# Half-width tiles for the state-space diagonal products, and later turns for the convolution's channels

## The chip, the core and the metric

The kernel runs on one core of a Trainium2 chip. The metric is the device time of one execution in microseconds (us), the median of several executions. Lower is better. The five engines of the core run side by side, each through its own list of instructions in order, and wait for each other by semaphores: TensorE (PE in the profile; PEld is its loading of the stationary operand), VectorE (DVE), ScalarE (ACT), GpSimd (POOL) and SyncE (SP), whose list here issues the transfers between the chip's memory and the core.

## What is computed

One layer of a hybrid decoder block on a sequence of 1024 tokens with 1024 features, in float32: a token-mixing sub-layer (stick-breaking attention beside a Mamba-2 state-space mixer), a cross-attention sub-layer and a gated feed-forward sub-layer. The change touches two places of the mixer, the causal convolution that makes its inputs and the "diagonal" product inside each chunk of 128 tokens:

```python
xbc = lax.conv_general_dilated(xbc, conv_w[:, None, :], window_strides=(1,),
    padding=[(SSM_CONV - 1, 0)], dimension_numbers=('NWC', 'WIO', 'NWC'),
    feature_group_count=SSM_CONV_DIM)
xbc = jax.nn.silu(xbc + conv_b)
xs, bm, cm = _split(xbc, (SSM_INNER, SSM_GROUPS * SSM_STATE, SSM_GROUPS * SSM_STATE))
...
cb = jnp.einsum('bclgn,bcsgn->bcgls', cc, bc)
y_diag = jnp.einsum('bcgls,bcgels,bcsgep->bclgep', cb, decay, xc)
states = jnp.einsum('bclgn,bcgel,bclgep->bcgepn', bc, decay_to_end, xc)
y_off = jnp.einsum('bclgn,bcgepn,bcgel->bclgep', cc, prev_states, jnp.exp(a_cs))
return (y_diag + y_off).reshape(b, l, h, p)
```

There are 2048 channels of x, in 32 heads of 64, and 512 channels each of B and C, in 4 groups; a group serves 8 heads. A sequence is 8 chunks.

## The kernel before

A float32 operand of a dense product is split into a high and a low part (the float32r type), and a product is three passes of the array: high by high, high by low, low by high. `acc3` (L211) does this over four blocks of the inner dimension, so one call is 12 passes of 512 columns.

**The projections with the convolution (from about 0.27 to 0.64 ms).** 18 pairs of 128-feature blocks are projected by a seven-product Strassen-Winograd scheme, `winograd_pair` (L222). Its first three products open three sums in PSUM: `pa_` with b11, `pc_` with t1, `pb_` with b21. The remaining four (t2, b22, t3, t4) add to `pa_` and `pc_`, and between them ACT and DVE copy or add the sums into the two output tiles `y`: the sum of the first product is copied out (L228) before t2 may add to it, that of the second (L230) before b22. The weights of a pair are loaded by SP, summed on POOL (L183 to L186), and split by ACT (L98) and DVE (L101). The PSUM pool has six rooms for these sums, that is two pairs, so TensorE's order lays the first half of a pair between the halves of the pair before.

Twelve of the 18 pairs are convolution pairs. For each of its two blocks `conv` (L659) takes the finished `y`, runs the four taps (ACT L661, three on DVE L663), the sigmoid (ACT L664) and the product (POOL L665) into a tile `acc`. The 20 blocks that hold x and B are then turned: `tail` (L647) transposes `acc` in eight 128x128 pieces on TensorE (L653) into two PSUM tiles `tr` (a pool of two), which ACT copies (L655) and SP stores (L656) to `xs_d` or `bt_d`. The other six pairs are gate pairs (`gate`, L673): a sigmoid and a store. `y` and `acc` take their rooms in turn from the pool `t4` of six, tag `b4`.

`pair` (L677) puts a pair together: weights, `y`, the seven products, then the turns of every block that is waiting in `pend` (filled by the pair before), then the copy of the last sum (L686) and the convolution or the gate. The order of each engine's list is made by a scheduler when the kernel is built, from the order of the source, the dependencies and its own estimates; `behind` (L204) forbids it to issue instructions ahead of a marked one. The last pair is a gate pair. At its place the last turn waiting is put behind the last product.

**The state-space chunks (about 1.10 to 1.43 ms).** 32 steps (4 groups by 8 chunks) run in a software pipeline: `prep` two steps ahead makes the decay matrices (`dec`, L1087, and `seg`, on ACT and DVE), `states` one step ahead updates the running state (`pst`), `outp` (L1120) makes the output, `flip` two steps behind turns it (`ptr`). Between them stand pieces of the memory projections and of `branch`, the output projection of the mixer (`mm<-oth`), which serve as filling for TensorE. In `outp`, the product with the earlier state is `po` (three passes of 512 columns), and the diagonal product is `pd`: for each of 8 heads the stationary operand is that head's 128x128 matrix in `seg`, and the moving operand a slice of `xs` in plain float32. The array takes a plain float32 product in two passes, so a step has 16 passes of `pd`. The slice of a head is its 64 columns and, except for head 0, the 32 columns before them; the heads run from 7 down to 0, so that what a product wrote too far down is written over by the next one.

Of the kernel before, what the change touches and what calls it, by code (L numbers as in the profile page):

```python
# [8 lines left out]
F32 = mybir.dt.float32  # L9
# [7 lines left out]
P = 128  # L17
S = 1024
# [3 lines left out]
HALF = 512  # L22
# [3 lines left out]
NH, HD = 16, 64  # L26
NG, GH = 4, 8
# [7 lines left out]
def hybrid_block(ctx, tc, a, out, dbg=None):  # L35
    nc = tc.nc
    V, A, G, T = nc.vector, nc.scalar, nc.gpsimd, nc.tensor
# [11 lines left out]
    def mk(pl, shape, dt, tag, bufs=None):  # L49
        uid[0] += 1  # L50
        kw = {} if bufs is None else {"bufs": bufs}
        return pl.tile(shape, dt, tag=tag, name=f"{tag}_{uid[0]}", **kw)
# [151 lines left out]
    def behind(marks):  # L204

        st = ExitStack()
        for m in marks:
            st.enter_context(tc.issue_after(m.ins))
        return st

    def acc3(ps, w, b, first, last, tiles=None):  # L211

        for k in range(4):
            bh, bl = (b[0][:, k, :], b[1][:, k, :]) if tiles is None else tiles[k]
            T.matmul(ps, w[0][:, k, :], bh, start=first and k == 0, stop=False, skip_group_check=True)  # L215
            T.matmul(ps, w[0][:, k, :], bl, start=False, stop=False, skip_group_check=True)  # L216
            ins = T.matmul(ps, w[1][:, k, :], bh, start=False, stop=last and k == 3, skip_group_check=True)  # L217
        return ins

    ends = []  # L220

    def winograd_pair(psp, ws, hb, y):  # L222


        wa11, ws1, ws2, wa12, ws3, ws4, wa22 = ws
        pa_, pc_ = mk(psp, [P, HALF], F32, "mm"), mk(psp, [P, HALF], F32, "mm")
        acc3(pa_, wa11, hb["b11"], True, False)
        A.activation(y[0][0], pa_, AF.Copy)  # L228
        acc3(pc_, ws1, hb["t1"], True, False)
        A.activation(y[1][1], pc_, AF.Copy)  # L230
        acc3(pa_, ws2, hb["t2"], False, False)
        A.activation(y[0][1], pa_, AF.Copy)
        pb_ = mk(psp, [P, HALF], F32, "mm")
        acc3(pb_, wa12, hb["b21"], True, True)
        V.tensor_tensor(y[0][0], y[0][0], pb_, ALU.add)
        acc3(pa_, ws3, hb["t3"], False, False)
        V.tensor_tensor(y[1][1], y[1][1], pa_, ALU.add)
        acc3(pc_, ws4, hb["b22"], False, True)
        V.tensor_tensor(y[0][1], y[0][1], pc_, ALU.add)
        ends.append(acc3(pa_, wa22, hb["t4"], False, True))  # L240
        return pa_
# [7 lines left out]
    with ExitStack() as pa:  # L249
        hp_ = pool(pa, "hT")  # L250
        hb = {n: tuple(mk(hp_, [P, 4, HALF], F32R, n + s) for s in "hl") for n in HB}
# [22 lines left out]
        with ExitStack() as p1:  # L274
# [7 lines left out]
            t4 = pool(p1, "t4x0", 4)  # L282
            tt = pool(p1, "tcomb", 6)
            psp = pool(p1, "ps1", 2, PSUM)
# [141 lines left out]
        with ExitStack() as p1:  # L426
# [4 lines left out]
            psp = pool(p1, "psz", 4, PSUM)  # L431
# [198 lines left out]
        with ExitStack() as p1:  # L630
# [3 lines left out]
            t4 = pool(p1, "t4b", 6)  # L634
            t2 = pool(p1, "t2c", 2)
            dts = mk(pool(p1, "dts"), [P, 2, S // 4], F32, "dts")
            psp = pool(p1, "psx0", 6, PSUM)
# [4 lines left out]
                    yield r.rearrange("p k b f -> p k (b f)"), w_in[kh * 512:(kh + 1) * 512, c0:c0 + 2 * P].rearrange("(k p) f -> p k f", p=P)  # L642
                return loads

            pend = []

            def tail(f, acc):  # L647
                dst = xs_d[f // 4][:, (f % 4) * P:(f % 4 + 1) * P] if f < 16 else bt_d[f - 16]
                for half in range(2):
                    pt = mk(ps1, [P, HALF], F32, "tr")  # L650
                    for c in range(4):
                        cc = half * 4 + c
                        T.transpose(pt[:, c * P:(c + 1) * P], acc[:, cc * P:(cc + 1) * P], ident)  # L653
                    st = mk(t2, [P, HALF], F32, "b2")
                    A.activation(st, pt, AF.Copy)  # L655
                    nc.sync.dma_start(dst[half * HALF:(half + 1) * HALF].rearrange("(c p) f -> p c f", p=P),  # L656
                                      st.rearrange("p (c f) -> p c f", f=P))
# [18 lines left out]

            def pair(c0, f, fin, npool):  # L677
                ws = winograd_weights(rp, sfp, swp, adjacent(c0), npool)
                y = [mk(t4, [P, S], F32, "b4") for _ in range(2)]
                ys = [[t[:, 0:HALF], t[:, HALF:S]] for t in y]  # L680
                p = winograd_pair(psp, ws, hb, ys)
                while pend:

                    with behind(ends[-1:] if f == gts[-1][1] and len(pend) == 1 else []):
                        tail(*pend.pop(0))
                A.activation(ys[1][0], p, AF.Copy)  # L686
                fin(f, y[0])
                fin(f + 1, y[1])

            jobs = [(C_X + f * P, f, conv) for f in list(range(16, 24, 2)) + list(range(0, 16, 2))]  # L690
            gts = [(C_GA + f * P, f, gate) for f in range(0, 16 - LATE_GATES, 2)]
# [21 lines left out]
            for i, j in enumerate(order):  # L713
                if i == 2:
                    dt_columns()
                pair(*j, 3 if i == 0 else 0)
            while pend:
                tail(*pend.pop(0))

            b12 = tuple(mk(hp_, [P, 4, HALF], F32R, "t1" + s) for s in "hl")  # L720
            for i in range(2):
# [14 lines left out]
        with ExitStack() as p2:  # L736
# [17 lines left out]
            marks, sig = [], []  # L754
# [174 lines left out]
            for m in range(NM):  # L929
                h, half = m // 2, m % 2  # L930
                hp, r = m // 4, m % 4
# [21 lines left out]
    with ExitStack() as p3:  # L953
# [8 lines left out]
        t4 = pool(p3, "s4p", 3)  # L962
# [27 lines left out]
        marks = []  # L990
# [129 lines left out]
        def outp(n):  # L1120
            g, c = divmod(n, NCH)
            d, gd = chk[n], grp[g]
            rows_ = slice(c * P, (c + 1) * P)
            seg, xs = d["seg"], d["xs"]
            zs = mk(t2, [P, HALF], F32, "s2")
            nc.sync.dma_start(zs, zs_d[rows_, g * HALF:(g + 1) * HALF])
            y = mk(t2, [P, HALF], F32, "s2")
            G.tensor_tensor(v3(y), v3(xs), dsk[:, g * GH:(g + 1) * GH].unsqueeze(2).to_broadcast([P, GH, HD]), ALU.mult)
            if c > 0:
                po = mk(ps, [P, HALF], F32, "po")  # L1130
                mm3(po, d["ch"], d["cl"], *gd["st", c], True, True)
                yo = mk(t2, [P, HALF], F32, "s2")
                V.tensor_tensor(v3(yo), v3(po), bc(eam, c, g), ALU.mult)
                G.tensor_tensor(y, y, yo, ALU.add)

            pd = mk(ps, [P, HALF], F32, "pd")
            for h in range(GH - 1, -1, -1):
                hs = slice(max(0, h * HD - 32), (h + 1) * HD)
                ins = T.matmul(pd[:, hs], seg[:, h, :], xs[:, hs], start=True, stop=True)
                if h == GH - 1:  # L1140
                    marks.append(ins)
            V.tensor_tensor(y, y, pd, ALU.add)
            V.tensor_tensor(y, y, zs, ALU.mult)
            junk = mk(jk, [P, HALF], BF16, "junk")
            ms = mk(stats, [P, 1], F32, "ms")
            A.activation(junk, y, AF.Square, scale=float(HALF) ** -0.5, accum_out=ms)

            A.activation(y, y, AF.Copy, scale=rstd_of(ms))
            d["y"] = y
# [176 lines left out]
    with ExitStack() as p4:  # L1326
# [16 lines left out]
        for i, (half, k) in enumerate((half, k) for half in range(2) for k in range(KT)):  # L1343
# [3 lines left out]
            t, t_ = [mk(t2, [P, HALF], F32, "m2") for _ in range(2)]  # L1347
# [12 lines left out]
        for f in range(KT):  # L1360
            whi, wlo, _ = first if f == 0 else branch_weights(f)
# [18 lines left out]
    marks = []  # L1380
# [29 lines left out]
    t4 = pool(xt4, "t4x", 3)  # L1410
    psx = ExitStack()
    psp = pool(psx, "psx", 2, PSUM)
# [41 lines left out]
    with ExitStack() as q2:  # L1454
# [17 lines left out]
        for m in range(2):  # L1472
            t = mk(t4, [P, D], F32, "x4")
# [81 lines left out]
    with ExitStack() as q4:  # L1555
# [22 lines left out]
        b11, b21 = hf[0]  # L1578
# [308 lines left out]
```

## Time and profile before

| | |
|---|---|
| Median of 3 executions | 2576.5 us (2574.12 to 2578.33) |
| The profiled execution: its own time | 2577.68 us |
| The profiled execution: span from first to last instruction | 2575.9 us |
| Mean granted TensorE clock | 0.993 |
| Busy: DVE, ACT, POOL | 1797.3 us (70%), 1132.1 us (44%), 852.9 us (33%) |

The profile is that of one execution. A busy time adds up the recorded durations of an engine's instructions. A matmul pass is recorded from its start to a modelled end, about 0.39 us for 512 columns, while the next one starts 0.23 us after it; the cost of a pass in a full stream is therefore read from the distance of starts, and a stop of TensorE from a distance that is longer than that. In a timeline the columns are start, duration, engine, line, operation, tiles, shapes and count; the bracket tells how long the engine was idle before, and who released it. A shape such as 128*64 gives the rows and columns of the array that the instruction uses.

### The profile page before, as it was taken

How to read it: one execution, taken by the hardware profiler on the slowest of the kernel's cores; microseconds unless marked ns; L12 is line 12 of the kernel's file. 1: busy time of each engine (PE TensorE's matmuls, PEld its weight loads, DVE VectorE, ACT ScalarE, POOL GpSimd, SP SyncE). 2: the span in 40 equal slices, each digit the busy share in tenths (PEclk: the TensorE clock that was granted, in tenths of full speed). 3: DMA queues.
4: the chain of work that ended last, by engine and by line, in shares of the span. 5: the costliest groups of instructions: out<-in, count | busy, mean ns of one | idle time of the engine just before them, and what ended most of it. 6: DMA issues, size and time to landing. Idle time of an engine off the chain costs nothing. (4 is left out here: it accounts for less than half of the span.)

```text
span 2575.9 us, 32333 instructions
## 1 busy us (share of the span) xinstructions
PE 2487.7 (97%) x11866; PEld 2057.5 (80%) x11866; DVE 1797.3 (70%) x2093; ACT 1132.1 (44%) x2023; POOL 852.9 (33%) x650
## 2 busy tenths in 40 slices
PE   7999999999999999998999999999999999999998
PEld 5788887887888878787888778887787888888876
DVE  7665777767577887697888664416459666666997
ACT  5333454554556665565554312314333333334343
POOL 3221644444112111254655050101114333323762
PEclk9999999999999999999999999999999999999999
DMA  7441433333443433365332572311232232224232
GB/s 245 150 127 58 147 121 98 105 106 107 134 111 90 119 100 98 107 205 159 104 93 79 171 237 74 131 49 34 98 111 70 78 95 74 90 90 164 99 131 98
DMA packets 255272, 293.44 MB, mean 114 GB/s; under 512 B 17024, under 2 KB 175241, under 8 KB 254987
## 3 DMA queue, kind: packets, MB, share of 16 engines
q1 hardware_dynamic: 255114, 291.40, 36.3%
q8 instruction: 93, 1.52, 0.2%
q14 instruction: 65, 0.52, 0.1%
HBM read 200.10 MB, written 74.45 MB: 107 GB/s over the span
## 5 line engine op out<-in xcount | busy, mean ns | idle before, releaser
L861 DVE TENSOR_TENSOR_SCAN n<-n,mask 128x128 f32<-128x128 f32 (+7 forms) x128 | 187.9, 1494 | 23.4 <-ACT n L860 22.1
L101 DVE TENSOR_TENSOR sw<-sf,sw 128x512 fp32r<-128x512 f32 x150 | 126.3, 855 | 69.5 <-ACT sw L98 69.2
L878 ACT ACTIVATE wth<-tr,mone 128x512 fp32r<-128x512 f32 x192 | 110.6, 585 | 82.9 <-PE tr L875 81.0
L98 ACT ACTIVATE sw<-sf 128x512 fp32r<-128x512 f32 x150 | 91.9, 626 | 108.6 <-PE mm L217 95.2
L183 POOL TENSOR_TENSOR sf<-wr,wr 128x512 f32<-128x512 f32 x38 | 60.1, 1582 | 237.6 <-DMA wr<-in_w_gu_dram 114.5
L879 DVE SCALAR_TENSOR_TENSOR wtl<-tr,wth 128x512 fp32r<-128x512 f32 x192 | 99.6, 544 | 49.8 <-ACT wth L878 49.7
L101 DVE TENSOR_TENSOR sw<-wr,sw 128x512 fp32r<-128x512 f32 x113 | 110.6, 980 | 27.3 <-ACT sw L98 27.2
L217 PE MATMUL mm<-h,sw 128*128 128x512 f32 x320 | 125.0, 392 | 1.8 <-DVE sw L101 1.8
L215 PE MATMUL mm<-h,sw 128*128 128x512 f32 x320 | 122.6, 391 | 2.9 <-ACT h L98 2.3
L216 PE MATMUL mm<-h,sw 128*128 128x512 f32 x320 | 125.3, 391 | 0.0
L98 ACT ACTIVATE sw<-wr 128x512 fp32r<-128x512 f32 x113 | 70.8, 629 | 120.9 <-PE mm L217 120.2
L663 DVE SCALAR_TENSOR_TENSOR b<-b,prmT,b 128x1023 f32<-128x1023 f32 (+2 forms) x72 | 107.4, 1494 | 11.1 <-ACT b L661 10.4
L94 POOL TENSOR_SCALAR v<-va 128x512 fp32r<-128x512 f32 x16 | 20.6, 1288 | 283.8 <-PE av L888 166.0
L860 ACT ACTIVATE n<-sc 128x512 f32<-128x512 f32 (+1 forms) x192 | 88.7, 494 | 45.5 <-PE tr L875 28.7
L152 POOL TENSOR_SCALAR rstd<-ms 128x1 f32<-128x1 f32 x74 | 26.4, 356 | 239.2 <-ACT x L1398 112.2
L104 PE MATMUL mm<-oth,bw 128*128 128x512 f32 x256 | 103.6, 405 | 1.4 <-DVE a L1198 1.3
L104 PE MATMUL p<-bw,h 128*128 128x512 f32 x256 | 98.9, 391 | 3.3 <-DVE x L1400 2.4
L106 PE MATMUL mm<-oth,bw 128*128 128x512 f32 x256 | 100.8, 394 | 0.1
L105 PE MATMUL mm<-otl,bw 128*128 128x512 f32 x256 | 100.5, 393 | 0.0
L106 PE MATMUL p<-bw,h 128*128 128x512 f32 x256 | 100.1, 392 | 0.0
L185 POOL TENSOR_TENSOR sf<-wr 128x512 f32<-128x512 f32 x38 | 63.4, 1668 | 110.3 <-DVE sw L101 110.3
L105 PE MATMUL p<-bw,h 128*128 128x512 f32 x256 | 99.8, 390 | 0.0
(616 smaller groups left out, 8101.3 us busy)
## 6 DMA issues: line engine op xcount, KB each, us to landing
wr<-in_w_gu_dram SPq DMA_DIRECT2D x80, 256.0 KB
wr<-in_w_in_dram SPq DMA_DIRECT2D x36, 512.0 KB
zr<-in_w_in_dram SPq DMA_DIRECT2D x28, 512.0 KB
gu_d<-t SPq DMA_DIRECT2D x44, 256.0 KB
wraw<-in_w_in_dram SPq DMA_DIRECT2D x20, 512.0 KB
zs_d<-zo SPq DMA_DIRECT2D x32, 256.0 KB
xs_d<-b SPq DMA_DIRECT2D x32, 256.0 KB
kl<-gt SPq DMA_DIRECT2D x64, 128.0 KB
```

What stands on the lines that cost most here:

```text
L98: A.activation(o, i, AF.Copy)
L101: eng.tensor_tensor(o, i, hi.bitcast(F32), ALU.subtract)
L104: first = T.matmul(ps, sh, mh, start=start, stop=False)
L105: T.matmul(ps, sh, ml, start=False, stop=False)
L106: T.matmul(ps, sl, mh, start=False, stop=stop)
L215: T.matmul(ps, w[0][:, k, :], bh, start=first and k == 0, stop=False, skip_group_check=True)
L216: T.matmul(ps, w[0][:, k, :], bl, start=False, stop=False, skip_group_check=True)
L217: ins = T.matmul(ps, w[1][:, k, :], bh, start=False, stop=last and k == 3, skip_group_check=True)
L663: V.scalar_tensor_tensor(acc[:, sh:], y[:, :S - sh], cw(3 - sh, f), acc[:, sh:], ALU.mult, ALU.add)
L861: V.tensor_tensor_scan(nt[:, 0:L][:, ::-1], nt[:, 0:L][:, ::-1], mask[:, S - L:][:, ::-1], 1.0, ALU.mult, ALU.max)
L878: A.activation(wh[:, t0 * P:], pt[:, t0 * P:], AF.Identity, bias=mone)
L879: V.scalar_tensor_tensor(wl[:, t0 * P:], pt[:, t0 * P:], -1.0, wh[:, t0 * P:].bitcast(F32), ALU.add, ALU.subtract)
```

## The change

**Convolution.** `winograd_pair` gets a callback. When it is given, the first three products are issued ahead of any copy, and the callback gets the last pass of the third. It puts the turns of the blocks that are `ripe` behind that pass, makes the waiting blocks (`pend`) ripe for the next pair, and only then takes the rooms for `y`. The turns of a convolution pair thus stand behind the third product of the second pair that follows, not after the products of the first pair that follows. The last pair still turns what is left.

**Diagonal product.** Each head's product is cut in two by output rows: columns 0 to 63 of the head's matrix are the stationary operand of one product, which writes PSUM partitions 0 to 63, and columns 64 to 127 that of another, which writes partitions 64 to 127. The moving slice is the 64 columns of the head alone.

```diff
-    def winograd_pair(psp, ws, hb, y):
+    def winograd_pair(psp, ws, hb, y, between=None):
         wa11, ws1, ws2, wa12, ws3, ws4, wa22 = ws
         pa_, pc_ = mk(psp, [P, HALF], F32, "mm"), mk(psp, [P, HALF], F32, "mm")
         acc3(pa_, wa11, hb["b11"], True, False)
+        if between is not None:
+            acc3(pc_, ws1, hb["t1"], True, False)
+            pb_ = mk(psp, [P, HALF], F32, "mm")
+            y = between(acc3(pb_, wa12, hb["b21"], True, True))
         A.activation(y[0][0], pa_, AF.Copy)
-        acc3(pc_, ws1, hb["t1"], True, False)
+        if between is None:
+            acc3(pc_, ws1, hb["t1"], True, False)
         A.activation(y[1][1], pc_, AF.Copy)
         acc3(pa_, ws2, hb["t2"], False, False)
         A.activation(y[0][1], pa_, AF.Copy)
-        pb_ = mk(psp, [P, HALF], F32, "mm")
-        acc3(pb_, wa12, hb["b21"], True, True)
+        if between is None:
+            pb_ = mk(psp, [P, HALF], F32, "mm")
+            acc3(pb_, wa12, hb["b21"], True, True)
         V.tensor_tensor(y[0][0], y[0][0], pb_, ALU.add)
...
-            pend = []
+            pend, ripe = [], []
...
             def pair(c0, f, fin, npool):
                 ws = winograd_weights(rp, sfp, swp, adjacent(c0), npool)
-                y = [mk(t4, [P, S], F32, "b4") for _ in range(2)]
-                ys = [[t[:, 0:HALF], t[:, HALF:S]] for t in y]
-                p = winograd_pair(psp, ws, hb, ys)
-                while pend:
-
-                    with behind(ends[-1:] if f == gts[-1][1] and len(pend) == 1 else []):
-                        tail(*pend.pop(0))
+                y, ys = [], []
+
+                def turns(third):
+                    for t in ripe:
+                        with behind([third]):
+                            tail(*t)
+                    ripe[:] = pend
+                    pend.clear()
+                    y.extend(mk(t4, [P, S], F32, "b4") for _ in range(2))
+                    ys.extend([t[:, 0:HALF], t[:, HALF:S]] for t in y)
+                    return ys
+
+                p = winograd_pair(psp, ws, hb, None, turns)
+                if f == gts[-1][1]:
+                    for i, t in enumerate(ripe):
+                        with behind(ends[-1:] if i == len(ripe) - 1 else []):
+                            tail(*t)
                 A.activation(ys[1][0], p, AF.Copy)
...
-            while pend:
-                tail(*pend.pop(0))
...
             for h in range(GH - 1, -1, -1):
-                hs = slice(max(0, h * HD - 32), (h + 1) * HD)
-                ins = T.matmul(pd[:, hs], seg[:, h, :], xs[:, hs], start=True, stop=True)
-                if h == GH - 1:
-                    marks.append(ins)
+                hs = slice(h * HD, (h + 1) * HD)
+                for j in range(2):
+                    r = slice(j * HD, (j + 1) * HD)
+                    ins = T.matmul(pd[r, hs], seg[:, h, r], xs[:, hs], start=True, stop=True)
+                    if h == GH - 1 and j == 0:
+                        marks.append(ins)
```

## The prediction, made before the changed kernel ran

> **What bounds the kernel now.** I read the page's totals first, then the busy time of the engines by stretches, then TensorE's timeline in the two stages that the change touches.
>
> ```profile
> span 2575.9 us, 32333 instructions
> PE 2487.7 (97%) x11866; PEld 2057.5 (80%) x11866; DVE 1797.3 (70%) x2093; ACT 1132.1 (44%) x2023; POOL 852.9 (33%) x650
> ```
>
> ```profile
> 427.80:431.20 3.40, 3.40 (x10) 2.62 (x9) 1.99 (x3) 3.40 (x7) 0.60 (x1) 0.50 0.61 153
> 345.00:650.00 305.00, 297.28 (x1368) 245.55 (x1367) 220.81 (x207) 161.29 (x244) 141.23 (x75) 0.99 0.36 111
> 1140.00:1180.00 40.00, 35.07 (x185) 28.79 (x184) 35.55 (x39) 22.89 (x39) 22.29 (x21) 1.00 0.58 186
> 1300.00:1340.00 40.00, 40.00 (x224) 34.40 (x223) 36.27 (x46) 19.48 (x38) 22.48 (x20) 1.00 0.31 87
> ```
>
> The columns of the second fence are the stretch, then the busy time of PE, PEld, DVE, ACT and POOL, then the granted clock, DMA share and GB/s. TensorE is the bound: 97% of the span, 297.28 of 305 us in the convolution, all of 40 us in the middle of the chunks. So a pass of the array added or saved there, or a stop removed, goes to the end almost whole. Two exceptions matter. From 1140 to 1180, VectorE (35.55 of 40) is as full as TensorE (35.07); a saved pass is worth little there. From 1300 to 1340 VectorE has 36.27 of 40, so TensorE can gain some 9% before VectorE binds.
>
> **The diagonal products.** Where the sixteen passes of one chunk stand, their loads, and the only half-width passes in the kernel:
>
> ```profile
> 1310.44 0.39 PE L106 MATMUL po<-sth,cl 128*128 128x512 f32 x1
> 1310.67 1.89 PE L1139 MATMUL pd<-s,s 128*128 128x96 f32 x16
> ...
> 1320.25 1.89 PE L1139 MATMUL pd<-s,s 128*128 128x96 f32 x16
> ```
>
> ```profile
> 1310.44 1.98 PEld L1139 LDWEIGHTS pd<-s,s 128*128 128x128 f32 x16
> 1312.34 0.19 PEld L104 LDWEIGHTS mm<-oth,bw 128*128 128x128 f32 x1
> ```
>
> ```profile
> L1139 PEld LDWEIGHTS pd<-s,s x512: 186/192/333, 1101.9 to 1427.3; 128*128 128x128 f32 x171
> L1139 PE MATMUL pd<-s,s x512: 243/275/421, 1102.1 to 1427.4; 128*128 128x96 f32 x149, 128*128 128x64 f32 x22
> ...
> L406 PEld LDWEIGHTS pdt<-b11h,wds x4: 133/134/135, 45.4 to 49.1; 128*64 128x64 f32 x4
> ```
>
> From the first load to the one behind the sixteenth are 1312.34 - 1310.44 = 1.90 us. The first load has to let the 512-column pass of `po` by (1310.67 - 1310.44 = 0.23), so the other fifteen distances are 1.67 / 15 = 0.111 us. A pass of 96 columns is far shorter than the 0.23 of 512, so I read 0.111 as the time to load 128 stationary columns: the loads, not the streaming, set the pace. All of it is 512 x 0.111 = 57 us.
>
> The change makes 256 products of two passes into 512 of two, 1024 passes, each with 64 stationary columns. A load of 64 columns is recorded with 134 ns against 192 for 128, so 58 ns less; against the 189 of other full loads, as at 1312.34, it is 55 less. If the loads still go one after another, a pass costs 0.111 - 0.055 = 0.056 to 0.053 us, and 1024 of them 54 to 57 us: 3 us less to nothing. I take 0.057, one ns above, for two more hand-overs per head: 1024 x 0.057 - 57 = **+1 us**. The moving 32 columns that fall away cost nothing now, since they stream under a load. The trace does not show a pass with both sizes at 64. Its lower bound is half, 0.028, if the two halves of the array load and run side by side; its upper bound 0.111, if a small pass costs as much as a full one (+57 us). I stay at the middle because 0.057 is the nearest row less a measured difference, and because nothing in the trace shows two loads abreast.
>
> Changing between full and half width looks free:
>
> ```profile
> 45.41 0.40 PE L216 MATMUL pv<-vl,b11h 128*128 128x512 f32 x1
> 45.64 0.39 PE L406 MATMUL pdt<-b11h,wds 128*64 128x512 f32 x1
> 45.87 0.39 PE L217 MATMUL pv<-vh,b11l 128*128 128x512 f32 x1
> ```
>
> One half-width pass between two full ones keeps the 0.23 us step. The Trainium skill, page "TensorEngine Tiling (Array Packing)", section "Tiling Modes", says that changing the tiling mode drains the array; this row disagrees for 512 columns, and no row shows it for 64. By the rule the sum would be that of the rival on emptying below.
>
> **The convolution's turns.** TensorE's stops in this stage:
>
> ```profile
> 421.05 0.39 PE L217 MATMUL mm<-t4h,sw 128*128 128x512 f32 x1
> ...
> 423.09 0.39 PE L217 MATMUL mm<-t4h,sw 128*128 128x512 f32 x1
> 426.76 1.09 PE L653 MATMUL tr<-ident,b 128*128 128x128 f32 x8 [3.29 <-POOL b L665]
> 427.61 0.59 PE L215 MATMUL mm<-b21h,sw 128*128 128x512 f32 x1
> ...
> 431.34 0.40 PE L215 MATMUL mm<-b21h,sw 128*128 128x512 f32 x1
> ```
>
> ```profile
> 596.14 0.39 PE L215 MATMUL mm<-t1h,sw 128*128 128x512 f32 x1
> 597.31 0.41 PE L653 MATMUL tr<-ident,b 128*128 128x128 f32 x2 [0.79 <-ACT b L655]
> ...
> 600.07 0.39 PE L217 MATMUL mm<-t1h,sw 128*128 128x512 f32 x1
> 600.62 0.50 PE L215 MATMUL mm<-t4h,sw 128*128 128x512 f32 x1 [0.17 <-DVE b L237]
> ...
> 627.36 0.39 PE L217 MATMUL mm<-t4h,sw 128*128 128x512 f32 x1
> 628.84 1.09 PE L653 MATMUL tr<-ident,b 128*128 128x128 f32 x8 [1.09 <-POOL b L665]
> 631.53 0.50 PE L215 MATMUL mm<-t2h,sw 128*128 128x512 f32 x1 [1.61 <-ACT b L228]
> ...
> 639.61 0.39 PE L217 MATMUL mm<-t3h,sw 128*128 128x512 f32 x1
> 640.77 0.50 PE L215 MATMUL mm<-t4h,sw 128*128 128x512 f32 x1 [0.78 <-DVE b L237]
> ```
>
> The nine steps from 421.05 to 423.09 take 2.04 us, 0.227 each. At 423 the turn waits for POOL's product: 426.76 - 423.09 - 0.23 = 3.44 us. The idle time halves the granted clock for 3.4 us behind it (0.50 in the first row of the stretches): nine steps from 427.61 to 431.34 take 3.73 us instead of 2.04, another 1.69. In the changed program this turn stands one product later, behind 12 more passes (2.72 us). So 0.72 us of the stop stay, too short, I think, for the clock. Gain 2.72 + 1.69 = 4.4 us.
>
> At 596 and 600 the stops are 1.17 - 0.23 = 0.94 and 0.55 - 0.23 = 0.32 us. In the changed program turns and first products stand between these instructions and what they wait for. Gain 1.3.
>
> At the end of the stage the last convolution pair and the last gate pair meet. Stops: 1.48 - 0.23 = 1.25 before the turn; 2.69 less the eight short passes (0.85, as from 426.76 to 427.61), 1.84 before t2; 1.16 - 0.23 = 0.93 before t4. Together 4.0 us. In the changed program the gate pair's t2 directly follows the convolution pair's t4. ScalarE's order there still has the copy of that pair's last sum and its first tap ahead of the copy that t2 waits for:
>
> ```profile
> 629.14 0.58 ACT L686 ACTIVATE b<-mm 128x512 f32<-128x512 f32 x1
> 629.76 1.24 ACT L661 ACTIVATE b<-b,prmT 128x1024 f32<-128x1024 f32 x1
> 630.91 0.58 ACT L228 ACTIVATE b<-mm 128x512 f32<-128x512 f32 x1
> ```
>
> That is 0.39 for the last pass, then 629.14 to 631.49 = 2.35, with two hand-overs of 0.04 some 2.8 us from the start of the last pass, a stop of 2.6. The stop before t4 goes, since a turn of 0.85 us now stands in it, and the turns that waited for POOL here have been moved behind three and four products. Gain 4.0 - 2.6 = 1.4. The convolution sums to 4.4 + 1.3 + 1.4 = **-7.1 us**. Its bounds are 10.8 - all stops and the slow clock, with the small ones at restarts - and the loss of the queue rival below. The number of transposes (160), copies (40) and stores (40) is unchanged.
>
> A later turn holds its two rooms of the six longer, and the copy of the first sum (L228) now waits until rooms are free. It is covered: in the changed order the next pair's first 36 passes (8.2 us at 0.227) stand between that copy and t2. Where the cover is missing, at the stage's end, I counted it.
>
> **Sum.** -7.1 + 1 = -6.1 us against the profiled execution's own 2577.68: 2571.6. That execution is 1.2 us above the median of 2576.5, so the forecast is 2570.4 us, said as **2570.5**.
>
> **The rivals.** *Halves side by side.* The two halves load and compute at the same time, so a chunk's `pd` falls from 1.78 to 0.9 us. For: the load sets the pace, and the halves have their own columns. Against: nothing in the trace. A chunk takes 1320.25 - 1310.67 = 9.58 us now; TensorE would need 8.7, VectorE needs 9.58 x 36.27 / 40 = 8.69, so both would bind and about half of 0.9 is had, in the 22 chunks behind 1225 us only. 22 x 0.45 = 10 us: 2576.5 - 7.1 - 10 = **2559**. The same page of the Trainium skill, section "Tiling Modes", says that tiles load and multiply independently; by it this is the case.
>
> *The small pass is dear* (slower). One mechanism: a load and a pass of 64 columns have a floor near that of the full one, in the 32 blocks of `pd`. The change breaks even at 0.0555 + 7.1/1024 = 0.063 us a pass; from 0.068 on it loses more than 0.2%. Halfway between 0.057 and 0.111, at 0.084: 2576.5 - 7.1 + 1024 x 0.084 - 57 = **2598**. For: 2048 instructions where 1024 were. Against: the measured 55 ns.
>
> *The array empties at each change of width.* In the changed program `pd` stands in 44 blocks, 88 changes. A pass is recorded with 275 ns and its successor starts after 111, so emptying costs about 0.16: 88 x 0.16 = 14, **2585**. Against: the row at 45.64.
>
> *The queue gives the convolution's gain back* (slower or the same). SP now has more stores of turns in a row, each waiting for ScalarE's copy of a later turn, ahead of the next pair's weight loads; POOL already waits for those. The tightest weights are ready 2.1 us early:
>
> ```profile
> POOL sf L183 <- DMA wr<-in_w_in_dram: 57.2, 13, 9.8
> ```
>
> ```profile
> 410.74 2.33 DVE L101 TENSOR_TENSOR sw<-wr,sw 128x512 fp32r<-128x512 f32 x1 [0.48 <-ACT sw L98]
> ...
> 415.15 0.39 PE L215 MATMUL mm<-b11h,sw 128*128 128x512 f32 x1
> ```
>
> Turns moved by 2.72 us leave 0.6 us late; eight such pairs cost 5 us, and one clock drop 1.7 with the 3 us idle that causes it: 2576.5 - 6.1 + 9.7 = **2580**.
>
> **How the numbers follow.** Forecast 0.36, side by side 0.22, dear pass 0.17, emptying 0.10, queue 0.15. The forecast's own range is 2566 to 2575. I set 2555 to 2594: it leaves out the lower third of the side-by-side case and half of the dear pass, under 2 in 10. About 0.2% (5.2 us) is what a measurement can tell from none. The forecast lies just beyond that, so 0.62 of it counts as faster; with nearly all of side by side and a little of the rest, faster is 0.45. Same is 0.35 of the forecast and a third of the queue case, 0.20; slower the rest, 0.35.
>
> **What would show it.** Distance of starts of the half-width loads: 0.057 for the forecast, 0.028 a pair for side by side, above 0.063 for the dear pass; a longer first step at each block for emptying. In 300 to 650 us: no stop over 1 us at the turns but one of 2.6 before the last pair's t2, no half clock, and no product waiting for L98 or L101. New waits of VectorE's kind in the chunks would mean that the saved passes were not the bound. The forecast is wrong if the chunks' stage changes by more than 3 us, or the convolution stage shortens by less than 4.

## The result, and the profile after

| | before | after |
|---|---|---|
| Median | 2576.88 us (6 runs, 2574.12 to 2578.33) | 2556.99 us (6 runs, 2554.28 to 2559.63) |
| Ratio after / before, 95% interval | | 0.9926 (0.9913 to 0.9938) |
| The profiled execution: span | 2575.9 us | 2555.4 us |
| Mean granted TensorE clock | 0.993 | 0.992 |

The changed kernel is 19.9 us faster by the medians, and 19.1 us (0.74%) by the ratio, which is the figure used below. The forecast was 6.1 us: the right direction, and a third of the size. The measured time lies near the lower end of the stated range, below the 2566 to 2575 us that the forecast's own mechanism allowed. The page's totals of the changed kernel:

```profile
span 2555.4 us, 33383 instructions
PE 2475.9 (97%) x12378; PEld 2033.6 (80%) x12378; DVE 1772.8 (69%) x2093; ACT 1133.7 (44%) x2023; POOL 853.9 (33%) x650
```

TensorE runs 512 passes more than before and is busy 12 us less. TensorE's timeline at one chunk's diagonal products, with the next chunk's in the last line, then the pieces' load and pass rows grouped by line (count: shortest, median and longest ns, first and last start):

```profile
1305.62 0.39 PE L106 MATMUL po<-sth,cl 128*128 128x512 f32 x1
1305.94 1.15 PE L1155 MATMUL pd<-s,s 128*64 128x64 f32 x32
1307.02 0.50 PE L104 MATMUL mm<-oth,bw 128*128 128x512 f32 x1
1307.35 0.39 PE L105 MATMUL mm<-otl,bw 128*128 128x512 f32 x1
...
1314.99 1.15 PE L1155 MATMUL pd<-s,s 128*64 128x64 f32 x32
```

```profile
L1155 PEld LDWEIGHTS pd<-s,s x1024: 132/138/138, 1097.7 to 1409.1; 128*64 128x64 f32 x171
L1155 PE MATMUL pd<-s,s x1024: 222/222/271, 1097.7 to 1409.1; 128*64 128x64 f32 x171
```

32 passes stand between 1305.94 and 1307.02, that is 1.08 us or 0.034 a pass with the block's edges. Passes one after another at the forecast's 0.057 would take 1.8 us. In the single records of that group the passes start in pairs, 7 ns apart; the second pair comes 107 ns after the first, and each later one 58 ns after the one before: the halves run side by side. The second reading is at the edges. From the last pass of `po` to the first of `pd` are 0.32 us where a step is 0.23, and from 1307.02 to 1307.35 again 0.33. The stretch from 1305.62 to 1307.35 is 1.73 us: 16 pairs at 0.058 are 0.93, two ordinary steps 0.46, and 0.34 is left for the two changes of width, 0.17 each on average. From this chunk to the next are 1314.99 - 1305.94 = 9.05 us; it was 9.58. The stage of the chunks lasts 1409.1 - 1097.7 = 311.4 us, where it was 1427.4 - 1102.1 = 325.3 us: 14 us.

The busy time by stretches of the changed kernel (PE, PEld, DVE, ACT, POOL, clock, DMA share, GB/s); the first and third answer to two of the rows shown of before:

```profile
345.00:650.00 305.00, 301.69 (x1393) 249.78 (x1392) 215.29 (x209) 161.47 (x243) 136.35 (x76) 0.99 0.37 112
...
1300.00:1340.00 40.00, 39.55 (x292) 31.97 (x291) 34.99 (x47) 22.64 (x44) 22.44 (x22) 1.00 0.36 104
626.90:631.40 4.50, 4.22 (x13) 3.32 (x13) 3.55 (x2) 1.66 (x3) 3.98 (x2) 0.68 0.00 2
```

In the convolution TensorE is busy 4.4 us more of the 305 (301.69 against 297.28). What stops are left, in its timeline:

```profile
425.10 0.39 PE L217 MATMUL mm<-t4h,sw 128*128 128x512 f32 x1
426.18 0.50 PE L215 MATMUL mm<-b21h,sw 128*128 128x512 f32 x1 [0.69 <-ACT b L702]
...
624.30 0.39 PE L217 MATMUL mm<-t4h,sw 128*128 128x512 f32 x1
627.18 0.50 PE L215 MATMUL mm<-t2h,sw 128*128 128x512 f32 x1 [2.49 <-ACT b L232]
...
628.84 0.63 PE L215 MATMUL mm<-t2h,sw 128*128 128x512 f32 x1
...
629.69 0.63 PE L217 MATMUL mm<-t2h,sw 128*128 128x512 f32 x1
```

Of the stop of 3.44 us at 423 are 1.08 - 0.23 = 0.85 us left, and the passes behind it go at full pace: no clock is lost. The stop at the stage's end is 2.88 - 0.23 = 2.65 us. About a microsecond and a half behind it the passes go in steps of 0.43 us in place of 0.23, and the granted clock of that stretch is 0.68: this stop does cost clock.

### The profile page after: what moved, and what is told of

It reads as the page before. It is cut to its first block, busy times and chain, and to the rows that moved or that the text cites. A ratio compares the mean times of both kernels' runs of the same rounds, so it can differ in the third digit from the quotient of the medians.

```text
span 2555.4 us, 33383 instructions
## 1 busy us (share of the span) xinstructions
PE 2475.9 (97%) x12378; PEld 2033.6 (80%) x12378; DVE 1772.8 (69%) x2093; ACT 1133.7 (44%) x2023; POOL 853.9 (33%) x650
## 5 line engine op out<-in xcount | busy, mean ns | idle before, releaser
L875 DVE TENSOR_TENSOR_SCAN n<-n,mask 128x128 f32<-128x128 f32 (+7 forms) x128 | 181.7, 1445 | 23.4 <-ACT n L874 22.2
L101 DVE TENSOR_TENSOR sw<-sf,sw 128x512 fp32r<-128x512 f32 x150 | 120.9, 818 | 82.0 <-ACT sw L98 80.5
```

The costliest lines, as they stand in the source:

```text
L101: eng.tensor_tensor(o, i, hi.bitcast(F32), ALU.subtract)
L875: V.tensor_tensor_scan(nt[:, 0:L][:, ::-1], nt[:, 0:L][:, ::-1], mask[:, S - L:][:, ::-1], 1.0, ALU.mult, ALU.max)
```

## The experiments

Each kernel was timed in 3 or 5 rounds beside the kernel before, on the same chip. The table gives the ratio to before with its 95% interval, the same as microseconds of 2576.5, and what the profile's pass rows give for the length of the chunks' stage (last less first start of `pd`).

| kernel | ratio | us against before | chunks' stage, us |
|---|---|---|---|
| convolution alone | 0.9981 (0.9971 to 0.9990) | -4.9 | 328.9 |
| tiles alone | 0.9947 (0.9935 to 0.9959) | -13.7 | 311.6 |
| both: the changed kernel | 0.9926 (0.9913 to 0.9938) | -19.1 | 311.4 |
| the same, lower halves first | 0.9981 (0.9972 to 0.9990) | -4.9 | 323.6 |
| the same, four tiles of 32 | 0.9972 (0.9962 to 0.9982) | -7.2 | 322.8 |
| the same, halves with 96 moving columns | 0.9982 (0.9973 to 0.9991) | -4.6 | 327.3 |
| the same, whole width with 64 moving columns | 0.9983 (0.9974 to 0.9992) | -4.4 | 329.9 |
| the same, two blocks a chunk | 0.9946 (0.9933 to 0.9960) | -13.9 | 313.9 |
| the same with a late copy | 0.9910 (0.9895 to 0.9926) | -23.2 | 311.6 |
| late copy, blocks kept whole | 0.9930 (0.9917 to 0.9944) | -18.0 | 311.3 |

**The two edits apart.** The first is the changed kernel with the old loop of `pd`, the second the kernel before with the new one.

```diff
-                hs = slice(max(0, h * HD - 32), (h + 1) * HD)
-                ins = T.matmul(pd[:, hs], seg[:, h, :], xs[:, hs], start=True, stop=True)
+                hs = slice(h * HD, (h + 1) * HD)
+                for j in range(2):
+                    r = slice(j * HD, (j + 1) * HD)
+                    ins = T.matmul(pd[r, hs], seg[:, h, r], xs[:, hs], start=True, stop=True)
```

> The kernel before with the convolution's edit alone; the diagonal products as before. Theory: the two edits add up, and the stage boundaries of the two traces tell their shares: the last turn of the convolution comes 2.7 us earlier although its first product starts 1.9 us later, so this kernel should be about 4.6 us below before, some 2572, and the rest of the 20 us is not in it. Rival: the convolution is worth the 7.1 us of the forecast (2569.7) and the difference is lost further on. Second rival: the later turns help the attention and chunk stages too (other buffers, other order), and this kernel has 10 us or more of the gain: 2567 or less.

> The kernel before with the diagonal products' edit alone; the convolution as before. Theory: the two halves load and run abreast, a pair each 58 ns, and each chunk's block is 0.5 us shorter: 32 x 0.5 = 16 us at most, 14 as the stage boundaries have it, so some 2563. Rival (the forecast's term): the loads go one after another and the edit costs 1 us: 2578; then the 14 us of the chunks came from the convolution's edit.

Measured: -4.9 and -13.7 us; their sum, -18.6, is the changed kernel's -19.1 well within the intervals. The edits add up, the tiles are three quarters of the gain, and the convolution is worth the 4.6 us of the stage boundaries rather than the 7.1 of the forecast, though its interval (2.6 to 7.5 us) just holds that too. Of the convolution alone the profiled execution (a span of 2575.8 us) is the longest of its twelve runs, so its time is read from the medians. The stage's length moves by some 4 us with the order of the lists alone (325.3 us before, 328.9 with the convolution's edit, with the same passes); only the step between 322 or more and 314 or less is read as more than that.

**Halves side by side, or small passes simply cheap?** All lower halves of a chunk, then all upper halves:

```diff
-            for h in range(GH - 1, -1, -1):
-                hs = slice(h * HD, (h + 1) * HD)
-                for j in range(2):
-                    r = slice(j * HD, (j + 1) * HD)
+            for j in range(2):
+                r = slice(j * HD, (j + 1) * HD)
+                for h in range(GH):
+                    hs = slice(h * HD, (h + 1) * HD)
```

> The changed kernel with the order of the 16 half products of a chunk turned: all eight lower halves, then all eight upper ones, so that a pass has a neighbour of its own half nearly everywhere. The number of passes, loads and changes of width is the same. Theory (abreast): two passes overlap only if they lie in different halves of the array, so the loads go one after another at about 0.057 us: a block is 32 x (0.057 - 0.029) = 0.9 us longer, 32 blocks 29 us, some 2585. Rival (a small pass is simply cheap, 0.029 us whatever its neighbour): no change, 2557.

TensorE's timeline at one chunk, and below it the waits of TensorE from 1095 to 1430 us by line and releaser (total us, times, longest), all that the profile names:

```profile
1300.35 0.39 PE L106 MATMUL po<-sth,cl 128*128 128x512 f32 x1
1300.66 1.90 PE L1155 MATMUL pd<-s,s 128*64 128x64 f32 x32
...
1302.83 0.39 PE L105 MATMUL mm<-otl,bw 128*128 128x512 f32 x1
```

```profile
PE mm L105 <- DVE bw L101: 2.3, 2, 1.7
PE mm L106 <- DVE bw L101: 0.7, 2, 0.4
PE pd L1155 <- DVE s L1158: 0.6, 1, 0.6
```

The stretch is 2.48 us against 1.73, so 0.75 us longer for the same 32 passes in another order: (2.48 - 0.34 - 0.46) / 32 = 0.053 on average, and 0.058 between neighbours of one half in the single records. Where the last lower halves of this chunk meet the first upper ones, three pairs of passes start 4 to 5 ns apart. They belong to different heads and move different columns of `xs`, so a shared moving operand is not what lets two passes run at once. It is the neighbour in the other half that makes a pass cheap, and a small pass next to its own kind costs what the forecast took, 0.057. At -4.9 us the kernel stands where the convolution alone stands: in this order the tiles bring nothing, as the forecast had it. The time rose by 14 us, not by the 29 expected. The waits say why: the longer blocks fill stops. They come to 3.6 us here, while the changed kernel's ten largest groups come to 11.7 (the first four are below).

```profile
PE dec L1101 <- ACT s L1102: 3.2, 5, 1.3
PE mm L105 <- DVE bw L101: 2.2, 2, 1.8
PE dec L1101 <- DVE cb L1078: 1.6, 1, 1.6
PE mm L104 <- ACT wraw L1252: 1.4, 2, 0.8
```

**What sets the 58 ns of a pair?** Four tiles of 32 columns halve the loads and keep the 64 moving columns; two tiles with the old slice keep the loads and stream 96; the whole width with 64 moving columns tests the forecast's word that the 32 extra columns cost nothing.

```diff
-                for j in range(2):
-                    r = slice(j * HD, (j + 1) * HD)
+                for j in range(4):
+                    r = slice(j * 32, (j + 1) * 32)
```

```diff
-                hs = slice(h * HD, (h + 1) * HD)
+                hs = slice(max(0, h * HD - 32), (h + 1) * HD)
```

```diff
-                for j in range(2):
-                    r = slice(j * HD, (j + 1) * HD)
-                    ins = T.matmul(pd[r, hs], seg[:, h, r], xs[:, hs], start=True, stop=True)
+                ins = T.matmul(pd[:, hs], seg[:, h, :], xs[:, hs], start=True, stop=True)
```

> The changed kernel with four tiles of 32 columns for each head in place of two of 64: 64 passes a chunk. Theory (the load of the stationary columns sets the pace, and tiles of different columns load abreast): four passes of 32 columns take half of what two of 64 take, 29 ns in place of 58; a block is 16 x 0.029 = 0.46 us shorter. VectorE's 8.69 us a chunk then bind near 9.05 - 0.36, so 8 to 12 us less: 2545 to 2549. Rival: the 64 moving columns, or the row of a tile, set the 58 ns: four passes per 58 ns, no change, 2557. Second rival: instructions are issued no faster than one per 29 ns, so a block is 32 x 0.029 = 0.93 us longer: 2587.

> The changed kernel, but the moving slice of a head is 96 columns again (32 more than needed, as before the change), in two half-width tiles. Theory, new since the run with quarters: not the load but the moving columns set the pace, about 0.86 ns a column; so a pair takes 0.083 us in place of 0.058, a block 16 x 0.025 = 0.40 us longer. That is 13 us of TensorE's time in 32 blocks, of which a part goes into the stops that the stage still has: the time 2562 to 2570. Rival (the forecast's view: the columns stream under the load and cost nothing): a pair stays at 0.058 us and the time at 2557.

> The changed kernel with the whole 128x128 matrix of a head as one stationary operand again, no tiles, but the moving slice cut to the head's own 64 columns. Theory (the moving columns set the pace): a pass takes about 0.084 us in place of 0.111, as the passes of head 0 did before, which had 64 columns; a block is 15 x 0.027 = 0.4 us shorter than before and has no change of width, so it stands at some 1.57 us against 1.40 with tiles and 1.93 before. The time is 0 to 5 us above the changed kernel, 2557 to 2562: most of the tiles' gain without tiles. Rival (the forecast's view: a load of 128 columns takes 0.111 us and hides the streaming): block and chunks as before, 14 us above the changed kernel, 2571.

TensorE's timeline at one chunk of each, in this order:

```profile
1303.27 0.39 PE L106 MATMUL po<-sth,cl 128*128 128x512 f32 x1
1303.59 1.10 PE L1155 MATMUL pd<-s,s 128*32 128x64 f32 x64
...
1304.96 0.40 PE L105 MATMUL mm<-otl,bw 128*128 128x512 f32 x1
```

```profile
1306.30 0.39 PE L106 MATMUL po<-sth,cl 128*128 128x512 f32 x1
1306.62 1.49 PE L1155 MATMUL pd<-s,s 128*64 128x96 f32 x32
...
1308.38 0.40 PE L105 MATMUL mm<-otl,bw 128*128 128x512 f32 x1
```

```profile
1306.55 0.39 PE L106 MATMUL po<-sth,cl 128*128 128x512 f32 x1
1306.78 1.89 PE L1153 MATMUL pd<-s,s 128*128 128x64 f32 x16
...
1308.79 0.39 PE L105 MATMUL mm<-otl,bw 128*128 128x512 f32 x1
```

The stretches are 1.69, 2.08 and 2.24 us, against 1.73 with halves. Four quarters take as long as two halves (a group of four each 56 ns in the single records), so the load doesn't set the pace of tiles. Halves with 96 columns take 0.35 us more, a pair each 83 ns: the moving columns set it, (0.083 - 0.058) / 32 = 0.8 ns a column. At whole width it is the other way round: 2.24 us is 16 x 0.111 plus two ordinary steps, the same as before with 96 columns, so the load sets the pace and the 32 columns were indeed free. My second theory, that the moving columns set the pace at whole width too, fell with this run. Together the four kernels that have the convolution's edit (whole width or halves, 64 or 96 columns) read -4.9, -4.4, -4.6 and -19.1 us: neither the cut to 64 columns nor the tiles bring anything alone. The halves with 96 columns have blocks 0.16 us shorter than the whole-width ones, 5.1 us in 32 chunks, and the time doesn't show it. The single records go most of the way to explain it: other passes split the half-width products into 44 blocks, 12 more than chunks, and 12 x 0.34 is 4.1 us. At whole width a split costs nothing: the six blocks of 8 passes in the trace of before take 1.35 us by the median, 8 x 0.111 and two ordinary steps. TensorE's list is also in another order here than in the changed kernel, and no run separates that.

With quarters the blocks are as short as with halves, yet the time is 11.9 us longer, where 8 to 12 us less was expected. TensorE's waits there, the three largest groups:

```profile
PE dec L1101 <- DVE cb L1078: 4.3, 2, 2.3
PE pd L1155 <- DVE s L1158: 3.1, 3, 1.4
PE dec L1101 <- ACT s L1102: 2.8, 4, 1.0
```

The ten largest come to 21.8 us, 10 more than in the changed kernel, and they are waits for VectorE and ScalarE. The scheduler, which has twice as many products to place, lays the lists in another order. That the order brings the waits is argued, not shown; it would take the changed kernel's order with quarters in it, which was not tried.

**Does a change of width empty the array?** `po` is put in the middle of the half-width passes, between heads 4 and 3:

```diff
+                if h == 3 and c > 0:
+                    with behind([ins]):
+                        sh, sl = gd["st", c]
+                        T.matmul(po, d["ch"], sh, start=True, stop=False)
+                        T.matmul(po, d["ch"], sl, start=False, stop=False)
+                        cut = [T.matmul(po, d["cl"], sh, start=False, stop=True)]
...
+                    with behind(cut):
+                        ins = T.matmul(pd[r, hs], seg[:, h, r], xs[:, hs], start=True, stop=True)
```

> The changed kernel with the product with the earlier state (three full-width passes of po) put in the middle of the half-width passes, so that a chunk has two blocks of them and four changes of width in place of two; nothing else is added. Theory (the array empties at a change): each more block costs about 0.2 us, 0.09 ahead of it and 0.11 behind it, 28 chunks 5.7 us of TensorE's time, and the time is 2560 to 2563. Rival (a change of width is free, as the forecast read it; the longer steps at a block's edges belong to the first load of plain float32 or to the profile): the sum of the two blocks' edges equals one block's, 2557.

```profile
1310.61 0.39 PE L106 MATMUL pst<-s2r,bl 128*128 128x512 f32 x1
1310.93 0.69 PE L1157 MATMUL pd<-s,s 128*64 128x64 f32 x16
1311.55 0.50 PE L1150 MATMUL po<-sth,ch 128*128 128x512 f32 x1
1311.88 0.39 PE L1151 MATMUL po<-stl,ch 128*128 128x512 f32 x1
1312.11 0.40 PE L1152 MATMUL po<-sth,cl 128*128 128x512 f32 x1
1312.44 0.69 PE L1157 MATMUL pd<-s,s 128*64 128x64 f32 x16
1313.05 0.50 PE L104 MATMUL mm<-oth,bw 128*128 128x512 f32 x1
1313.39 0.39 PE L105 MATMUL mm<-otl,bw 128*128 128x512 f32 x1
```

Each half block has the edges of a whole one: 1311.88 - 1310.61 = 1.27 us, less 8 x 0.058 and two ordinary steps is 0.35; 1313.39 - 1312.11 = 1.28 us gives 0.35 again. A whole-width block has none (2.24 us above is passes alone). The time is 0.0020 of 2576.5, some 5 us, above the changed kernel's, inside the expected range, with intervals that overlap a little. The trace has 68 blocks against 44 there, and 24 x 0.34 is 8 us; TensorE's waits in the stage fell from 11.7 us to 4.9, and the stage is only 2.5 us longer. So the rows, not the time, show the price of a change of width: 0.17 us. That the array empties there is the likely reason; the rows show only the price.

**The stop at the convolution's end.** The copy of the last sum of the last convolution pair, and the convolution of its second block, move behind the two copies that the gate pair's t2 and b22 wait for:

```diff
         A.activation(y[1][1], pc_, AF.Copy)
+        while held:
+            held.pop(0)()
...
+                if (c0, f, fin) == order[-2]:
+                    fin(f, y[0])
+
+                    def rest():
+                        A.activation(ys[1][0], p, AF.Copy)
+                        fin(f + 1, y[1])
+
+                    held.append(rest)
+                    return
```

(The second block joins the last turns: `ripe.extend(pend)` ahead of their loop.)

> The changed kernel with one more edit in the convolution: ScalarE's copy of the last sum of the last convolution pair, and the convolution of that pair's second block, stand behind the two copies that the last gate pair's t2 and b22 wait for. Theory: the stop of 2.65 us before that t2 shrinks to the copies alone, about 0.6 us from the end of the pass, so 1 us or less is left of it, and the half clock of 3 us behind it goes too (1.4 us): 2.5 to 4 us less, 2553 to 2554.5. Rival: the second block's taps, product and turns come that much later, the turns are the last work of the stage, and the stop moves behind the last product: no change, 2557, with a stop of some 2 us before the last eight turns.

The busy time by stretches of this kernel:

```profile
345.00:650.00 305.00, 304.17 (x1413) 252.51 (x1412) 211.98 (x206) 163.31 (x246) 138.45 (x78) 1.00 0.38 115
626.00:631.00 5.00, 4.86 (x26) 3.89 (x25) 4.70 (x5) 3.43 (x5) 0.26 (x1) 1.00 0.47 133
```

TensorE is busy 304.17 of the 305 us, against 301.69, and the clock stays at 1.00 where it was 0.68. The time is 4.1 us below the changed kernel's by the ratios. Since the two intervals overlap, both kernels ran once more on one chip:

> The kernel with the late copy once more, next to the changed kernel on the same chip, since the two intervals against the kernel before (0.9895 to 0.9926 and 0.9913 to 0.9938) touch. Theory: the stop and the half clock that the late copy takes away are worth 4 us, so it stays 3 to 5 us below the changed kernel. Rival: the first pair of runs differed by the chip, and the two agree within 1.5 us.

> The changed kernel once more, next to the late copy on the same chip. Theory: 3 to 5 us above the late copy, and some 0.9925 of the kernel before, as at first. Rival: within 1.5 us of the late copy.

Late copy 2552.39 us (ratio 0.9911, 0.9897 to 0.9924), changed kernel 2558.39 (0.9935, 0.9922 to 0.9949): 6 us apart, with intervals that touch. Over both occasions the medians are 2552.5 us in 8 runs and 2557.5 us in 11, and only two of the 8 lie above the shortest of the 11. The traces agree: from the stage's first product (`mm<-b11h,sw`) to the attention's first (`av`) are 404.4 and 403.8 us with the late copy, 407.9 and 407.8 without. So the late copy is faster than the changed kernel, by some 4 us.

**Fewer blocks.** In the changed kernel's trace the half-width passes of the 32 chunks stand in 44 blocks, split by a `dec` pass or by filling. The first half-width pass of a chunk is put behind the second `dec` pass of the two chunks that follow:

```diff
-                T.matmul(pe, f4["keys"][:, cs], cr[:, hs, :], start=True, stop=True)
+                d["dec"] = T.matmul(pe, f4["keys"][:, cs], cr[:, hs, :], start=True, stop=True)
...
+                    with behind([chk[m]["dec"] for m in (n + 1, n + 2) if m in chk] if h == GH - 1 and j == 0 else []):
```

> The kernel with the late copy, and each chunk's half-width passes kept in one block: the first of them is put behind the second dec pass of the two chunks that follow, which in a dozen chunks stood between them. Theory (each block costs two changes of width, about 0.3 us over a whole-width block): a dozen blocks fewer, 3 to 4 us of TensorE's time; the wait that some of these dec passes have now stands ahead of the block instead of inside it and loses the cover of 6 to 14 passes, 0.2 to 0.4 us in six places, 2 us back. Sum 1 to 3 us less than with the late copy alone: about 2550 beside 2552.5, a ratio to before of 0.990 to 0.9905. Rival: the waits of the dec passes set the chunks' pace and the block's edges lie in their shadow: no change, 0.991.

A miss, and past the rival as well: 2556.44 us, 4 us more than with the late copy alone, with intervals that overlap a little. The trace has 37 blocks in place of 44. Where one such block stood, first with the late copy, then kept whole:

```profile
1243.35 0.68 PE L1168 MATMUL pd<-s,s 128*64 128x64 f32 x14
1245.91 0.50 PE L1114 MATMUL dec<-colrows,keyrows 128*128 128x512 f32 x1 [1.88 <-DVE cb L1091]
1246.34 0.80 PE L1168 MATMUL pd<-s,s 128*64 128x64 f32 x18
```

```profile
1249.45 0.50 PE L1114 MATMUL dec<-colrows,keyrows 128*128 128x512 f32 x1 [1.32 <-DVE cb L1091]
1249.88 1.15 PE L1169 MATMUL pd<-s,s 128*64 128x64 f32 x32
```

The wait for VectorE stays (1.88, 1.32 us), now ahead of the block. The chunks' stage is 311.3 us against 311.6, so fewer blocks bring nothing there. But this length is counted from the first `pd`, and the edit itself puts that pass back, behind two `dec` passes:

```profile
1094.01 0.49 PE L104 MATMUL pst<-s2r,bh 128*128 128x512 f32 x1 [0.62 <-ACT state L1136]
1095.18 0.70 PE L1114 MATMUL dec<-colrows,keyrows 128*128 128x512 f32 x2 [0.68 <-DMA colrows<-sum_d]
1095.82 1.15 PE L1169 MATMUL pd<-s,s 128*64 128x64 f32 x32
```

In the trace of the late copy the first block's passes stand ahead of these two instructions, and neither has a wait. Counted from the attention's last product (`av`), the first `pd` comes after 12.9 us against 9.9, and the last `pd` after 324.1 us against 321.5. So 2.6 of the 4 us are lost by the end of the chunks, out of sight of the table's measure; which wait brings them, and where the rest is lost, was not settled.

## Why the prediction was right in direction and short in size

By the signs that the prediction named for itself, its mechanism failed: the chunks' stage changed by 14 us, where 3 was the limit (the convolution's, which had to shorten by 4 us or more, did so by 4.6). The measured time lies in the stated range only because that range was drawn to take in part of the side-by-side rival.

- **Diagonal products: +1 us forecast, -13.7 measured.** The step that failed is "if the loads still go one after another", taken "because nothing in the trace shows two loads abreast". The trace of before could not show it: no two neighbouring passes there lay in different halves. That was no evidence against it, and the case was priced as a rival. The price of a single small pass, 0.057, was right in size, as the run with the lower halves first shows (0.058); two of them abreast cost that once. It was worked out as the time of a load, though, and in tiles the moving columns set the pace (next point): that the size was right is luck.
- **"The loads, not the streaming, set the pace"** was right at whole width, and so was "the moving 32 columns cost nothing now" (the whole-width run with 64 columns). Carried over to tiles it was wrong: there the moving columns set the pace, and the two facts only look alike because 64 columns happen to stream in 58 ns.
- **"Changing between full and half width looks free"** was wrong, by 0.17 us a change. The row it was read from has one tile of 64 columns at column 0 and 512 moving columns; what sets it apart from the two tiles here was not tried. The rival on emptying had 0.16 us, read from the 275 ns of a pass. The prediction weighed this rival and the side-by-side one as if they excluded each other. They hold together: a whole block saves 16 x (0.111 - 0.058) = 0.85 us and gives 0.34 back, 0.51 net, and the 9.58 us between neighbouring chunks became 9.05. Over the 44 blocks that the 32 chunks stand in, 32 x 0.85 - 44 x 0.34 = 12.2 us; measured are 13.7 (10.6 to 16.7). The Trainium skill, page "TensorEngine Tiling (Array Packing)", section "Tiling Modes", has both rules, that a change of mode drains the array and that tiles load and multiply independently. The chunks' rows agree with both (0.17 us a change, starts 7 ns apart); the row at 45.64 does not show the first.
- **VectorE as the bound** was overrated. The side-by-side rival took half of the gain, in 22 chunks, because VectorE would need 8.69 us a chunk. In the same stretch from 1300 to 1340 it is busy 34.99 of 40 us in place of 36.27, TensorE still 39.55. Its share in one stretch was no floor for a chunk: the other half of the gain went into the changes of width. That this rival's 2559 lies only 2 us from the result is luck as well, since its 10 us for the chunks are 4 too few and the 7.1 for the convolution 2 too many.
- **Convolution: -7.1 us forecast, -4.9 measured** (-4.6 by the stage's boundaries). The places were right: 0.85 us left at 425 where 0.72 was forecast and no clock lost there, and 2.65 us before the last pair's t2 where 2.6 was forecast. The mis-sized term is that last one, "4.0 - 2.6": the prediction itself priced the half clock behind a long stop at 1.69 us, and did not charge it to a stop of 2.6 us. It cost some 1.5 us, seven steps of 0.43 in place of 0.23 and a partial one. The late copy, which takes the stop away, gets some 4 us.
- **The other rivals** fell. The small pass is not dear. The queue did not give the gain back: from 300 us to the end of the convolution the changed kernel's timeline shows two waits of TensorE, those at 426.18 and 627.18, both for ScalarE's copy of a sum, and none for a weight.
- **The sum.** Of the 13 us between the forecast's -6.1 and the -19.1 by the ratio, the diagonal products explain 14.7 (from +1 to -13.7), and the convolution takes 2.2 back.

## What to carry to other kernels

When the stationary operand is loaded anew for every short product, cut it into column tiles and let neighbouring passes lie in different tiles: order decides, since the same tiles in blocks of their own half lost 14 us, all that the tiles had brought. Cut the moving operand to what is needed at the same time, since in tiles it sets the pace, and count 0.17 us for each change of width, so keep the narrow passes together, unless that moves a wait out of its cover. And price every stop of TensorE with the clock that it costs behind it: here 0.85 us cost none, 2.65 us about 1.5 and 3.44 us about 1.7. Length alone does not decide it. In the trace of before, a stop of 2.57 us (from the pass at 1832.15 to that at 1834.95, less a step) keeps the full clock behind it, while one of 2.46 us (1956.63 to 1959.32) is followed by a lower one; the granted clock is the third number from the end:

```profile
1835.00:1839.00 4.00, 4.00 (x18) 3.27 (x19) 1.81 (x2) 1.15 (x2) 0.80 (x2) 1.00 0.32 131
1959.20:1963.20 4.00, 3.88 (x11) 3.11 (x12) 4.00 (x8) 1.22 (x3) 0.00 (x0) 0.65 0.00 0
```

What sets the two apart is not shown.

## What was not expected of the hardware

- A plain float32 pass in a half-width tile is paced by its moving columns (0.058 us with 64, 0.083 with 96), one at whole width by its load (0.111 with either).
- Loads of 32 columns, four abreast, bring nothing over loads of 64, two abreast: 56 against 58 ns a head and pass.
- 24 us of added passes (0.75 us in 32 chunks) cost only 14: TensorE's waits in the stage fell from 11.7 us to 3.6. An engine that is 97% busy still has room at the places where it waits.
